# A two-layer hybrid decoder trunk on one core: loads of the decays by chunk, two products of the second layer moved into the end of the first, and operands of the way out ordered by halves of the tokens

## The chip, the cores and the metric

One core of one Trainium2 chip. A core has five engines that run side by side, each through its own instructions in order: TensorE (PE; its weight loads are listed as PEld), VectorE (DVE), ScalarE (ACT), GpSimd (POOL) and SyncE (SP), which here only issues DMA. The metric is the time of one execution in microseconds of the device (us); the comparison is of medians of runs.

## The reference

Two residual layers with RMSNorm and a last RMSNorm, on 1024 tokens of width 1024, all in float32. The first ("even") layer has dilated attention and an HGRN2 recurrence behind one projection; the second ("odd") is a gated DeltaNet with 8 key heads and 16 value heads. Cut to what the change touches:

```python
def forward(x):                                   # (1, 1024, 1024)
    h = x + even_mixer(rms_norm(x, norm_w[0]))    # ends in: concat(a, b) @ w_out
    h = h + odd_mixer(rms_norm(h, norm_w[1]))
    return rms_norm(h, final_norm_w)

def odd_mixer(hn):
    qkv, z, b_logit, a_logit = split(hn @ w_in)   # b_logit, a_logit: 16 columns each
    q, k, v = split(silu(causal_conv4(qkv)))
    g = -exp(a_log) * softplus(a_logit + dt_bias); gcum = cumsum(g within a chunk)
    decay = exp(where(causal, gcum_i - gcum_j, -inf))
    a_mat = I + where(strict, (k beta) @ k.T * decay, 0)      # solved per chunk and head
    ...                                           # delta rule over the chunks
    return (rms_norm(o) * silu(z)) @ w_out
```

## The kernel before

**Products.** Each float32 operand is split into `hi` (an ACT cast to fp32r) and `lo` (a DVE subtraction, `cut`, line 345); a product is three matmuls (`mm3`, line 382). Weights come in units of four loads of 256 KB through two `raw` buffers into seven `hi` and seven `lo` buffers; `unit()` (line 371) hands out a unit and loads the next. Accumulators of projections lie in two PSUM banks `pj`.

**Even layer** (line 555). Its way out, `out_proj` (line 491), goes through eight groups of 256 rows of the mixed activations, which lie in DRAM (`ymix`) and are cut into operands by `y_steps` (line 537) in four loads: two blocks of 128 rows (c) by two halves of 512 tokens. The first group of the even way out (`lead`) starts with tokens 512 to 1023; the other groups start with token 0. In the last group the finished tokens go on at once: the residual's sum on DVE, `norm_T` (line 449: square and root on ACT, scaling on DVE, eight transposes `nt` on PE, cast `hn_hi` on ACT, subtraction `hn_lo` on DVE). The order here is the framework's, by its estimates.

**Odd layer** (line 1049). All its operations are collected and put in order by `Plan` (line 82), a list scheduler with costs per operation; it takes 430 ns of SP and 3100 ns to the landing for every load (line 124), and holds a tile back until its predecessor in the same buffer is free (gates, line 212). The order it finds is what each engine then executes. `gates()` (line 1061) makes the cumulated decays: `ab`, a product of 32 columns (`abp`, half by half), a turn (`abt`), then ACT and DVE steps, and at the end a table `gcd` of 64 KB in DRAM, a row of 128 floats per chunk (8) and value head (16). `start()` (line 1511) makes the first keys (`pk0`, then `conv`), `proj(j)` the others. For each of the 8 key heads `invert(hh)` (line 1295) loads rows of `gcd` to all 128 partitions as L, two chunks of two heads per load; ACT does four Relu (one per chunk and head) and one exp per load; DVE multiplies L with `kk` from PE, a PSUM bank `c` per four chunks, of which there is one; then follow the inverse and `recur(hh)` (line 1397), which loads the same rows again by chunk as A (`decays`, line 1289), for POOL to add a mask. `invert(hh + 1)`, the projections and the gate products run as filling between the steps of `recur(hh)`. All loads and stores are issued by SP.

Of the kernel before, what the change touches and what calls it, by code (L numbers as in the profile page):

```python
# [10 lines left out]
F32 = mybir.dt.float32  # L11
# [8 lines left out]
P = 128  # L20
# [3 lines left out]
KC = D // P  # L24
# [57 lines left out]
class Plan:  # L82
# [87 lines left out]
    def edges(self):  # L170
# [28 lines left out]
        for op in ops:  # L199
            i = op["i"]  # L200
            for ap, w in [(z, True) for z in op["out"]] + [(z, False) for z in op["ins"]]:
                t = ap.tensor
# [9 lines left out]
        tags = {}  # L212
        for t, users in tiles.values():
            if getattr(t, "tag_meta", None) is not None:
                tags.setdefault((t.tag, t.tag_meta.bufs), []).append((t.owner_uid, sorted(set(users))))
        gates = []
        for (tag, bufs), ts in tags.items():
            ts.sort(key=lambda z: z[0])
# [93 lines left out]
def trunk_kernel(ctx: ExitStack, tc: tile.TileContext, x, ew, ewo, ow, owab, owo, nw, fnw, lbl, hnw,  # L312
# [13 lines left out]
    def bank(tag, shape, name):  # L326
        return pp.tile(shape, F32, name=name, tag=tag, bufs=BANKS[tag])
# [43 lines left out]
    def unit(first=lambda: None):  # L371
        w = ahead.pop() if ahead else load_unit()
        first()
        ahead.append(load_unit())
        return w
# [36 lines left out]
    def drain(fill):  # L412
        for _ in fill:
            pass
# [8 lines left out]
    def hn(part, k, s):  # L423
        return HN[part][k // 4][:, k % 4, s]
# [24 lines left out]
    def norm_T(src, t, sm, nwb, xn):  # L449
# [3 lines left out]
        for h in range(2):  # L453
# [4 lines left out]
            act.copy(hi, ps)  # L458
            dve.tensor_tensor(HN["lo"][h][:, :, t * 128:(t + 1) * 128], ps, hi.bitcast(F32), op=ALU.subtract)

    def proj_cols(w, c, name, evac, halves=(0, 1), mid=None):

        w = by_k(w[2 * c:2 * c + 2], 128)
        for half in halves:
            ps = bank("pj", [P, 512], f"{name}_{half}")
            s = slice(half * 512, half * 512 + 512)
            for k, (hi, lo) in enumerate(w):
                mm3(ps, hi, lo, hn("hi", k, s), hn("lo", k, s), k == 0, k == KC - 1)
                if k == KC - 1:
                    if mid and half == 0:  # L470
                        mid()
                    evac(s, ps)
                if k % 2:
                    yield 1.3
# [16 lines left out]
    def out_proj(groups, y_parts, hres, after, tags, lead=0.0, spread=False):  # L491
# [1 line left out]

        n_ = 0
        y = [y_parts(groups[0])]
        drain(y_steps(*y[0]))
        for g in groups:
            yh, yl = y.pop()[:2]
            steps = iter(())
# [34 lines left out]
                yield 1.3  # L534
            drain(steps)

    def y_steps(yh, yl, row, then=None):

        for c in range(2):
            for half in range(2):  # L540
                n = slice(half * 512, half * 512 + 512)
                cut(ymix[row + c * 128:row + c * 128 + 128, n], yh[c][:, n], yl[c][:, n], f"y{row}_{c}_{half}")
                yield
        if then:
            then()
# [9 lines left out]
    def even_layer(es):  # L555
# [482 lines left out]
            drain(fill)  # L1038
        open_stage("wy", WAY)
        drain(out_first(range(4, 8), ["pj", "b"]))  # L1040
        stage.close()

    with ExitStack() as es:
# [5 lines left out]
    def odd_layer(es):  # L1049
# [11 lines left out]
        def gates():  # L1061
# [7 lines left out]
            load_row(dt, dtb)  # L1069
            load_row(ea, alog)  # L1070
            act.activation(ea, ea, AF.Exp)

            w = unit().rearrange("p (k j) -> p k j", k=KC)
            ab = sp.tile([P, T], F32, name="ab", tag="LpQ")
            for half in range(2):
                p = bank("pj", [P, 512], f"abp{half}")
                s = slice(half * 512, half * 512 + 512)
                for k in range(2):
                    for r in range(4):
                        for part in ("hi", "lo"):  # L1080
                            pe.matmul(p[32 * r:32 * r + 32], w[:, 2 * r + k], hn(part, 2 * r + k, s).bitcast(F32),
                                      start=k == 0 and part == "hi", stop=k == 1 and part == "lo")
                act.copy(ab[:, s], p)
                yield (9 if not half else 0.0), 2.6
            yield 1.0, 0.0
            tp = bank("c", [P, NT, 32], "abt")
            for c in range(NT):
# [198 lines left out]
                    gated(7, e, h, G7[0][:, e, h, :])  # L1286
                    yield 0.7, 0.4

        def decays(hh, c):
            g = sp.tile([P, 2, 128], F32, name=f"A{hh}_{c}", tag="A", bufs=4)  # L1290
            sync.dma_start(g, bass.AP(tensor=gcd.tensor, offset=gcd.offset + (c * 16 + 2 * hh) * 128,
                                         ap=[[0, P], [128, 2], [1, 128]]))
            return g

        def invert(hh):
            kT = KT[hh]
# [3 lines left out]

            for c in range(0, NT, 2):

                sync.dma_start(L[:, 2 * c:2 * c + 4, :],
                               bass.AP(tensor=gcd.tensor, offset=gcd.offset + (c * 16 + 2 * hh) * 128,
                                       ap=[[0, P], [16 * 128, 2], [1, 256]]))
                for u in range(4):
                    act.activation(L[:, 2 * c + u, :], L[:, 2 * c + u, :], AF.Relu,
                                   bias=gt["ngc"][:, c + u // 2, 2 * hh + u % 2:2 * hh + u % 2 + 1])
                act.activation(L[:, 2 * c:2 * c + 4, :], L[:, 2 * c:2 * c + 4, :], AF.Exp, scale=-1.0)
# [87 lines left out]
        def recur(hh):  # L1397
# [2 lines left out]
            ss = SS[hh] = sp.tile([P, NT, 2], F32, name=f"oss{hh}", tag="oss", bufs=2)  # L1400

            def decay_a(c):
                DA = decays(hh, c)
                pool.tensor_tensor(DA, DA, MA[:, None, :].to_broadcast([P, 2, 128]), op=ALU.add)
                for e in range(2):
                    act.activation(DA[:, e, :], DA[:, e, :], AF.Exp, bias=gt["ngc"][:, c, 2 * hh + e:2 * hh + e + 1])
                return DA
# [101 lines left out]
                yield from g  # L1509

        def start():
            yield from conv(unit(), 0, 8, "k0", lambda: k_tile(0))
            yield from proj(0)

        fill = blend(plan.early(10000, gates()), start())
# [83 lines left out]
```

## Time and profile before

| | us |
|---|---|
| median of three runs | 2263.21 (2261.76 to 2263.47) |
| the profiled execution, its own time | 2265.53 |
| its span, from the first to the last instruction | 2263.8 |
| PE busy | 2159.7 |
| DVE busy | 1410.1 |
| ACT busy | 943.2 |
| mean granted clock of PE, share of full speed | 0.980 |

The page of the profile gives busy times, a picture of the span in 40 slices, DMA queues, the chain of work that ended last and groups of instructions. Matmuls overlap in the records: the spacing of their starts is the pace. In rows of a timeline the brackets hold the idle time before an instruction and what ended it; a wait that ends with a load names the load. L291 and L305 are the lines of the planner's and the lanes' calls, so that tiles, not lines, tell what an instruction is. The granted clock has two levels, 1.00 and 0.50 (2.4 and 1.2 GHz); a value between them is a mean over a stretch.

### The profile page before, as it was taken

Reading aid. Unit: us, or ns where it says so; the run is one execution under the profiler, and the core shown is the slowest. Engines: PE = TensorE matmul, PEld = TensorE weight load, DVE = VectorE, ACT = ScalarE, POOL = GpSimd, SP = SyncE. Lnnn points to the kernel's source line nnn. Section 1 sums busy time; section 2 is a strip of 40 time slices with the busy share of each in tenths; the row PEclk is TensorE's granted clock in tenths of the full one; section 3 lists DMA queues with packets and bytes.
Section 4 is the critical chain, followed back from the end, with each engine's and each line's share of the span. In section 5 each row is a group of like instructions: output and inputs, shape, how many; then the busy total and the mean of one; then the engine's idle time right before and its main releaser. Section 6 shows DMA issues by size and latency. Waiting matters only on the chain. (4 is left out here: it accounts for less than half of the span.)

```text
span 2263.8 us, 52378 instructions
## 1 busy us (share of the span) xinstructions
PE 2159.7 (95%) x21781; PEld 1777.9 (79%) x21781; DVE 1410.1 (62%) x3236; ACT 943.2 (42%) x2519; POOL 240.7 (11%) x252
## 2 busy tenths in 40 slices
PE   7999999999999999979998898989899999999998
PEld 6888888888877878757886786868787787887887
DVE  6353535353444344457675896969788787965677
ACT  6233333333232232222235755655565555553223
POOL 0010101010000000000000012121212122220100
PEclk9999999999999999989999999999999999999999
DMA  4111111114342334353222312231211222223223
GB/s 147 39 48 48 48 48 44 48 34 129 89 130 73 106 92 122 98 162 105 91 102 96 87 44 42 80 71 54 76 53 68 60 66 54 78 73 144 94 95 119
DMA packets 99566, 184.14 MB, mean 81 GB/s; under 512 B 12160, under 2 KB 29696, under 8 KB 99328
## 3 DMA queue, kind: packets, MB, share of 16 engines
q1 hardware_dynamic: 99328, 180.79, 26.4%
q8 instruction: 171, 2.80, 0.5%
q14 instruction: 67, 0.55, 0.1%
HBM read 151.25 MB, written 29.49 MB: 80 GB/s over the span
## 5 line engine op out<-in xcount | busy, mean ns | idle before, releaser
L305 DVE TENSOR_TENSOR w_lo<-raww,w_hi 128x512 fp32r<-128x512 f32 x160 | 117.8, 740 | 150.9 <-ACT w_hi L305 150.4
L305 ACT CAST w_hi<-raww 128x512 fp32r<-128x512 f32 x160 | 99.3, 621 | 204.2 <-DMA raww<-in_ewo_dram 54.2
L291 PE MATMUL op<-w_hi,yplo 128*128 128x512 f32 x448 | 140.1, 391 | 0.7 <-DVE hr L291 0.7
L305 ACT ACTIVATE P<-P,nm 128x256 f32<-128x256 f32 (+7 forms) x128 | 71.4, 559 | 133.8 <-DVE nm L305 133.7
L291 ACT CAST w_hi<-raww 128x512 fp32r<-128x512 f32 x132 | 81.3, 618 | 92.4 <-DMA raww<-in_owo_dram 38.1
L291 DVE TENSOR_TENSOR hr<-hr,op 128x512 f32<-128x512 f32 x128 | 87.4, 686 | 48.4 <-PE op L291 46.0
L305 PE MATMUL op<-w_hi,yphi 128*128 128x512 f32 x320 | 105.6, 403 | 9.9 <-DVE hres L305 6.6
L291 PE MATMUL oz<-hn_hi,w_hi 128*128 128x512 f32 x256 | 110.9, 433 | 0.0
L291 DVE TENSOR_TENSOR w_lo<-raww,w_hi 128x512 fp32r<-128x512 f32 x132 | 95.0, 724 | 24.6 <-ACT w_hi L291 22.4
L291 PE MATMUL pv<-hn_hi,w_hi 128*128 128x512 f32 x256 | 108.2, 422 | 0.0
L291 PE MATMUL oz<-hn_lo,w_hi 128*128 128x512 f32 x256 | 105.1, 410 | 0.0
L291 PE MATMUL oz<-hn_hi,w_lo 128*128 128x512 f32 x256 | 103.6, 405 | 0.0
L291 PE MATMUL pv<-hn_lo,w_hi 128*128 128x512 f32 x256 | 103.2, 403 | 0.0
L291 PE MATMUL pv<-hn_hi,w_lo 128*128 128x512 f32 x256 | 102.8, 402 | 0.0
L291 POOL TENSOR_TENSOR A<-A,MA 128x256 f32<-128x256 f32 x64 | 53.4, 836 | 447.7 <-DMA A<-gcd 217.5
L305 DVE STREAM_TRANSPOSE PB<-P 128x256 f32<-128x256 f32 (+3 forms) x64 | 54.6, 853 | 72.8 <-ACT P L305 72.8
L291 PEld LDWEIGHTS op<-w_hi,yplo 128*128 128x128 f32 x448 | 84.1, 188 | 18.3 <-DVE hr L291 0.9
L291 PE MATMUL op<-w_lo,yplo 128*128 128x512 f32 x224 | 87.2, 389 | 0.0
L305 DVE TENSOR_TENSOR hres<-hres,op 128x512 f32<-128x512 f32 x96 | 64.6, 682 | 31.2 <-PE op L305 30.4
L305 PEld LDWEIGHTS op<-w_hi,yphi 128*128 128x128 f32 x320 | 61.5, 193 | 26.0 <-DVE hres L305 7.8
L305 DVE CUSTOM_DVE_ANT_0 P<-S,G 128x256 f32<-128x256 f32 (+7 forms) x128 | 58.1, 491 | 36.5 <-PE S L305 36.1
L291 DVE SCALAR_TENSOR_TENSOR vT<-uv,cws,vT 128x512 f32<-128x512 f32 x96 | 73.7, 769 | 4.6 <-ACT vT L291 2.9
(345 smaller groups left out, 6348.8 us busy)
## 6 DMA issues: line engine op xcount, KB each, us to landing
raww<-in_ew_dram SPq DMA_DIRECT2D x128, 256.0 KB, 3.1
raww<-in_ow_dram SPq DMA_DIRECT2D x100, 256.0 KB, 3.0
V<-vd SPq DMA_DIRECT2D x64, 256.0 KB, 5.4
rawy<-ymix SPq DMA_DIRECT2D x64, 256.0 KB, 2.7
raww<-in_ewo_dram SPq DMA_DIRECT2D x32, 256.0 KB, 3.0
L<-gcd SPq DMA_DIRECT2D x32, 256.0 KB, 11.7
A<-gcd SPq DMA_DIRECT2D x64, 128.0 KB, 2.9
ymix<-oy SPq DMA_DIRECT2D x32, 256.0 KB, 2.4
```

The costliest lines, as they stand in the source:

```text
L291: ops[i]["f"](*ops[i]["a"], **ops[i]["kw"])
L305: return f(*a, **kw)
```

## The change

L's rows of `gcd` are loaded chunk by chunk: two loads of 128 KB where one of 256 KB brought two chunks; the Relu and exp steps stay. At the end of the even layer, behind its way out, the unit of `ab` and the unit of the first keys are taken (which loads that unit and the next), and the first halves of the two products are made: `ab` and `pk0`, tokens 0 to 511, each left in its `pj` bank. The odd layer copies them from there and makes the second halves; its planner no longer has those two products and the eight weight loads. The gates' first step now hands 5.0 instead of 9 units of filling to the blend. `y_steps` cuts by halves of the tokens first, and by blocks of rows inside; the first group with `lead` begins with the second half. The planner sorts the tiles of a tag by the number in their name.

```diff
@@ -212,7 +212,7 @@
         tags = {}
         for t, users in tiles.values():
             if getattr(t, "tag_meta", None) is not None:
-                tags.setdefault((t.tag, t.tag_meta.bufs), []).append((t.owner_uid, sorted(set(users))))
+                tags.setdefault((t.tag, t.tag_meta.bufs), []).append((int(t.name.rsplit("_", 1)[1]), sorted(set(users))))
         gates = []
         for (tag, bufs), ts in tags.items():
             ts.sort(key=lambda z: z[0])
@@ -458,12 +458,34 @@
             act.copy(hi, ps)
             dve.tensor_tensor(HN["lo"][h][:, :, t * 128:(t + 1) * 128], ps, hi.bitcast(F32), op=ALU.subtract)
 
+    def ab_half(w, half):
+
+        w = w.rearrange("p (k j) -> p k j", k=KC)
+        p = bank("pj", [P, 512], f"abp{half}")
+        s = slice(half * 512, half * 512 + 512)
+        for k in range(2):
+            for r in range(4):
+                for part in ("hi", "lo"):
+                    pe.matmul(p[32 * r:32 * r + 32], w[:, 2 * r + k], hn(part, 2 * r + k, s).bitcast(F32),
+                              start=k == 0 and part == "hi", stop=k == 1 and part == "lo")
+        return p
+
+
+    begun = {}
+
     def proj_cols(w, c, name, evac, halves=(0, 1), mid=None):
 
         w = by_k(w[2 * c:2 * c + 2], 128)
         for half in halves:
+            s = slice(half * 512, half * 512 + 512)
+            ps = begun.pop((name, half), None)
+            if ps is not None:
+                if mid and half == 0:
+                    mid()
+                evac(s, ps)
+                yield 1.3
+                continue
             ps = bank("pj", [P, 512], f"{name}_{half}")
-            s = slice(half * 512, half * 512 + 512)
             for k, (hi, lo) in enumerate(w):
                 mm3(ps, hi, lo, hn("hi", k, s), hn("lo", k, s), k == 0, k == KC - 1)
                 if k == KC - 1:
@@ -493,7 +515,7 @@
 
         n_ = 0
         y = [y_parts(groups[0])]
-        drain(y_steps(*y[0]))
+        drain(y_steps(*y[0], first=1 if lead else 0))
         for g in groups:
             yh, yl = y.pop()[:2]
             steps = iter(())
@@ -534,10 +556,10 @@
                 yield 1.3
             drain(steps)
 
-    def y_steps(yh, yl, row, then=None):
-
-        for c in range(2):
-            for half in range(2):
+    def y_steps(yh, yl, row, then=None, first=0):
+
+        for half in (first, 1 - first):
+            for c in range(2):
                 n = slice(half * 512, half * 512 + 512)
                 cut(ymix[row + c * 128:row + c * 128 + 128, n], yh[c][:, n], yl[c][:, n], f"y{row}_{c}_{half}")
                 yield
@@ -1038,6 +1060,12 @@
             drain(fill)
         open_stage("wy", WAY)
         drain(out_first(range(4, 8), ["pj", "b"]))
+
+        begun["ab"] = unit()
+        begun["ab", 0] = ab_half(begun["ab"], 0)
+        begun["k"] = unit()
+        proj = proj_cols(begun["k"], 0, "pk0", lambda s, ps: begun.update({("pk0", 0): ps}), (0,))
+        drain(proj)
         stage.close()
 
     with ExitStack() as es:
@@ -1069,19 +1097,13 @@
             load_row(dt, dtb)
             load_row(ea, alog)
             act.activation(ea, ea, AF.Exp)
-
-            w = unit().rearrange("p (k j) -> p k j", k=KC)
             ab = sp.tile([P, T], F32, name="ab", tag="LpQ")
+            w = begun.pop("ab")
             for half in range(2):
-                p = bank("pj", [P, 512], f"abp{half}")
+                p = begun.pop(("ab", half), None) or ab_half(w, half)
                 s = slice(half * 512, half * 512 + 512)
-                for k in range(2):
-                    for r in range(4):
-                        for part in ("hi", "lo"):
-                            pe.matmul(p[32 * r:32 * r + 32], w[:, 2 * r + k], hn(part, 2 * r + k, s).bitcast(F32),
-                                      start=k == 0 and part == "hi", stop=k == 1 and part == "lo")
                 act.copy(ab[:, s], p)
-                yield (9 if not half else 0.0), 2.6
+                yield (5 if not half else 0.0), 2.6
             yield 1.0, 0.0
             tp = bank("c", [P, NT, 32], "abt")
             for c in range(NT):
@@ -1286,11 +1308,9 @@
                     gated(7, e, h, G7[0][:, e, h, :])
                     yield 0.7, 0.4
 
-        def decays(hh, c):
-            g = sp.tile([P, 2, 128], F32, name=f"A{hh}_{c}", tag="A", bufs=4)
+        def decays(g, hh, c):
             sync.dma_start(g, bass.AP(tensor=gcd.tensor, offset=gcd.offset + (c * 16 + 2 * hh) * 128,
                                          ap=[[0, P], [128, 2], [1, 128]]))
-            return g
 
         def invert(hh):
             kT = KT[hh]
@@ -1300,9 +1320,8 @@
 
             for c in range(0, NT, 2):
 
-                sync.dma_start(L[:, 2 * c:2 * c + 4, :],
-                               bass.AP(tensor=gcd.tensor, offset=gcd.offset + (c * 16 + 2 * hh) * 128,
-                                       ap=[[0, P], [16 * 128, 2], [1, 256]]))
+                decays(L[:, 2 * c:2 * c + 2, :], hh, c)
+                decays(L[:, 2 * c + 2:2 * c + 4, :], hh, c + 1)
                 for u in range(4):
                     act.activation(L[:, 2 * c + u, :], L[:, 2 * c + u, :], AF.Relu,
                                    bias=gt["ngc"][:, c + u // 2, 2 * hh + u % 2:2 * hh + u % 2 + 1])
@@ -1400,7 +1419,8 @@
             ss = SS[hh] = sp.tile([P, NT, 2], F32, name=f"oss{hh}", tag="oss", bufs=2)
 
             def decay_a(c):
-                DA = decays(hh, c)
+                DA = sp.tile([P, 2, 128], F32, name=f"A{hh}_{c}", tag="A", bufs=4)
+                decays(DA, hh, c)
                 pool.tensor_tensor(DA, DA, MA[:, None, :].to_broadcast([P, 2, 128]), op=ALU.add)
                 for e in range(2):
                     act.activation(DA[:, e, :], DA[:, e, :], AF.Exp, bias=gt["ngc"][:, c, 2 * hh + e:2 * hh + e + 1])
@@ -1509,7 +1529,7 @@
                 yield from g
 
         def start():
-            yield from conv(unit(), 0, 8, "k0", lambda: k_tile(0))
+            yield from conv(begun.pop("k"), 0, 8, "k0", lambda: k_tile(0))
             yield from proj(0)
 
         fill = blend(plan.early(10000, gates()), start())
```

## Rows read from the trace of the kernel before

**Rows 1.** Part 1 of the page: busy time of each engine, its share of the span of 2263.8 us, and its instructions.
```profile
PE 2159.7 (95%) x21781; PEld 1777.9 (79%) x21781; DVE 1410.1 (62%) x3236; ACT 943.2 (42%) x2519; POOL 240.7 (11%) x252
```
**Rows 2.** The waits of PE from 1150 us to the end: who waited for whom, us in total, times, longest us.
```profile
PE kk L291 <- DVE L L291: 30.2, 12, 6.6
PE up L291 <- issue: 8.4, 1, 8.4
PE ot L291 <- POOL bv L291: 5.5, 1, 5.5
```
**Rows 3.** The timelines of ACT (three rows), DVE and PE (one each) in the train of L loads of the fifth head, 1582 to 1608 us: start, us, engine, line, operation, out<-in, shapes, and in brackets the idle time before it and what ended it.
```profile
1592.55 0.40 ACT L291 ACTIVATE L<-L,g_ngc 128x128 f32<-128x128 f32 x1 [0.43 <-DMA L<-gcd]
...
1597.93 0.40 ACT L291 ACTIVATE L<-L,g_ngc 128x128 f32<-128x128 f32 x1 [3.58 <-DMA L<-gcd]
...
1599.05 0.61 ACT L291 ACTIVATE uq<-q 128x512 f32<-128x512 f32 x1
1599.70 0.69 DVE L291 SCALAR_TENSOR_TENSOR q<-uq,q 128x512 f32<-128x512 f32 x1 [4.17 <-ACT uq L291]
1600.71 0.80 PE L291 MATMUL kk<-kT 128*128 128x128 f32 x2 [5.65 <-DVE L L291]
```
**Rows 4.** The timelines of ACT and PE in the trains of the next three heads, in the same columns: for each the release of the second load, of the third load, and PE's wait.
```profile
1699.29 0.40 ACT L291 ACTIVATE L<-L,g_ngc 128x128 f32<-128x128 f32 x1 [1.29 <-DMA L<-gcd]
...
1703.23 0.40 ACT L291 ACTIVATE L<-L,g_ngc 128x128 f32<-128x128 f32 x1 [2.14 <-DMA L<-gcd]
...
1706.00 0.79 PE L291 MATMUL kk<-kT 128*128 128x128 f32 x2 [4.91 <-DVE L L291]
...
1804.46 0.40 ACT L291 ACTIVATE L<-L,g_ngc 128x128 f32<-128x128 f32 x1 [1.24 <-DMA L<-gcd]
...
1810.06 0.40 ACT L291 ACTIVATE L<-L,g_ngc 128x128 f32<-128x128 f32 x1 [3.79 <-DMA L<-gcd]
...
1812.83 0.79 PE L291 MATMUL kk<-kT 128*128 128x128 f32 x2 [6.65 <-DVE L L291]
...
1911.73 0.40 ACT L291 ACTIVATE L<-L,g_ngc 128x128 f32<-128x128 f32 x1 [1.32 <-DMA L<-gcd]
...
1915.57 0.40 ACT L291 ACTIVATE L<-L,g_ngc 128x128 f32<-128x128 f32 x1 [2.04 <-DMA L<-gcd]
...
1918.34 0.80 PE L291 MATMUL kk<-kT 128*128 128x128 f32 x2 [5.13 <-DVE L L291]
```
**Rows 5.** Busy time by stretches at the border of the two layers: from:to, length, then PE, PEld, DVE, ACT and POOL busy with their instructions, granted clock of PE, share of the DMA engines, GB/s.
```profile
1193.70:1205.50 11.80, 9.04 (x57) 3.83 (x56) 7.35 (x11) 4.51 (x12) 0.00 (x0) 0.98 0.11 46
1205.50:1211.10 5.60, 1.89 (x8) 1.78 (x8) 1.33 (x5) 3.25 (x5) 0.00 (x0) 0.50 0.51 139
1211.10:1220.00 8.90, 8.89 (x31) 7.16 (x32) 2.91 (x5) 2.58 (x5) 0.00 (x0) 0.77 0.45 148
```
**Rows 6.** Parts 5 and 6 of the page. First two groups of instructions, the cast and the subtraction that make a weight's pair of operands (count, then busy us and mean ns, then idle before them); then two groups of loads (count, KB of each, median us from issue to landing).
```profile
L305 DVE TENSOR_TENSOR w_lo<-raww,w_hi 128x512 fp32r<-128x512 f32 x160 | 117.8, 740 | 150.9 <-ACT w_hi L305 150.4
L305 ACT CAST w_hi<-raww 128x512 fp32r<-128x512 f32 x160 | 99.3, 621 | 204.2 <-DMA raww<-in_ewo_dram 54.2
...
L<-gcd SPq DMA_DIRECT2D x32, 256.0 KB, 11.7
A<-gcd SPq DMA_DIRECT2D x64, 128.0 KB, 2.9
```
**Rows 7.** The views by tile: L from 1583 to 1608 us (four loads of one train), then A from 1259 to 1275 us (three loads behind the first train).
```profile
DMA to landing us min/median/max: 5.7/11.1/14.6
DMA to landing us min/median/max: 5.8/7.7/10.1
```
**Rows 8.** The timeline of SP's queue, 1582 to 1608 us and 1259 to 1275 us: start of the first issue, us to the end of the last, what, and how many.
```profile
1583.46 1.92 SPq L291 DMA_DIRECT2D L<-gcd  x4
...
1261.84 5.86 SPq L291 DMA_DIRECT2D A<-gcd  x3
```
**Rows 9.** The chain of work that ended last, three of its pieces: start, us, what, and how many instructions it merges.
```profile
1220.79 3.67 PE abp L291 x32
...
1485.89 8.39 issue
...
1542.18 2.75 PE pk L291 x12
```
**Rows 10.** Groups of instructions by line from 1193.7 to 1220 us: count, busy us and mean ns, idle before.
```profile
L291 PE MATMUL abp<-hn_lo,wab 128*32 128x512 f32 x16 | 4.0, 595 | 0.0
```
**Rows 11.** The timelines of PE (two rows), DVE and SP's queue at the border of the layers, 1180 to 1212 us.
```profile
1204.18 1.24 PE L305 MATMUL nt<-ident,xn 128*128 128x128 f32 x8 [2.68 <-DVE xn L305]
1208.74 1.89 PE L291 MATMUL abt<-gcs__14227,ab 128*128 128x32 f32 x8 [3.32 <-DMA gcs__14227<-in_dtb_dram]
...
1205.60 1.22 DVE L305 TENSOR_TENSOR hn_lo<-nt,hn_hi 128x512 fp32r<-128x512 f32 x2
...
1205.50 0.81 SPq L291 DMA_DIRECT2D gcs__14227<-in_cst_dram  x2
```
**Rows 12.** The timelines of PE (two rows) and DVE (one) at the start of the even layer's way out, 975 to 1000 us.
```profile
982.99 0.80 PE L305 MATMUL op<-w_hi,yphi 128*128 128x512 f32 x1 [2.75 <-ACT yphi L305]
...
994.93 0.79 PE L305 MATMUL op<-w_hi,yphi 128*128 128x512 f32 x1 [6.62 <-DVE hres L305]
...
993.59 0.69 DVE L305 TENSOR_TENSOR yphi<-rawy,yphi 128x512 fp32r<-128x512 f32 x1 [8.00 <-ACT yphi L305]
```

## Prediction

> **What bounds the kernel now.** I read the page first: TensorE (PE) is busy for 2159.7 of 2263.8 us [rows 1]. So a microsecond is won only where PE stands still or runs at its lower clock, and the second view is PE's waits. Behind 1150 us they are few and long. The largest, 30.2 us, is the product `kk` of `invert`, which waits for VectorE's (DVE) work on L; one of 8.4 us is put down to nothing ("issue"), and one of 5.5 us is for GpSimd (POOL) [rows 2]. The third view is the timeline around the four longest `kk` waits, which come once per head from the fifth head on. The reader is to see one chain there. ScalarE (ACT) runs in order and stands at the first Relu of L's third load, released at 1597.93; the tanh `uq<-q` behind it starts at 1599.05, DVE's `q` at 1599.70, and PE's `kk` at 1600.71 after 5.65 us of standing still [rows 3]. The same order returns three times with waits of 4.91, 6.65 and 5.13 us [rows 4]: 22.3 us in the four heads. The fourth view is the border between the layers, by stretches: from 1193.7 to 1220.0 us PE has 31 `pk` products, 32 `abp`, 24 transposes and 8 `abt` to do; it is busy for 19.8 of 26.3 us, and its clock is at the lower level (0.50, that is 1.2 GHz) from 1205.5 to 1211.1 [rows 5].
>
> **L's decays by chunk.** Removed: 32 loads of 256 KB; added: 64 of 128 KB, the same bytes. Alone, loads of this size from `gcd` (the A loads) land in 2.9 us in the median, the 256 KB ones in 11.7 [rows 6]. That is no saving of 8.8 us per load, for the four stand in a row: in one train they landed 5.7 us (the shortest) to 14.6 us (the longest) after their issue [rows 7], the last being issued some 1.4 us after the first [rows 8]; so a train moves 1 MB in about 16 us, and eight halves of it are still 1 MB. I take the rate of these rows and let a chunk land where half of its pair had. What is then won is the wait for the pair's other half. Chunk 4 opens the third pair. It lands half way between the second and the third release, and the chain of [rows 3] hangs on it: (1597.93 - 1592.55) / 2 = 2.7 us, and in the next three 2.0, 2.8 and 1.9 us [rows 3, 4]. Sum 9.4 us. All four are less than the waits they shorten (4.9 us and more), so they reach PE whole, if ACT's order stays. For the other heads' smaller `kk` waits (30.2 - 22.3 = 7.9 us) I take 1 us. The 8.4 us of "issue" and the wait for POOL I leave: the first falls inside a train (from 1485.89) and shows no releaser [rows 9], the second hangs on an A load behind a train, whose end doesn't move. **10.4 us.** The price: SP issues 32 loads more, 0.4 to 0.5 us each, in the same train in which the ring is full anyway; who is queued behind them on SP is the A load, and before it a weight load in some heads.
>
> Bounds: the nearest rows for a train of small loads are three A loads, issued from 1261.84 on, the last one finished issuing at 1267.70; they took 10.1, 7.7 and 5.8 us [rows 7, 8], so they landed within about 1 us of each other, 0.5 us apart. Eight chunks at that pace behind a first one of 2.9 us are in at 6.5 us; chunk 4 is there at 5 us, before the first pair of today, and the 22.3 us go whole, with 4 to 8 us more in the first heads: 30. At the other end every chunk costs the lone 2.9 us: chunk 4 at 14.5 us, when today's third load is released (1597.93 - 1583.46 = 14.5), and the last at 23.2 instead of 16.0. I take the rate of the trains because the A loads of [rows 8] were behind other loads, which had cleared the way for them. So from 30 us won to 25 us lost (priced with the rivals), with 10.4 won in between.
>
> The Trainium skill ("DMA: Bandwidth & Descriptors", section "Rules for kernel authors") speaks against this edit: many small transfers are to be coalesced into one large one; the page's fit, 2.0 us fixed plus bytes over 436 GB/s (for another path of issue), makes 2.6 us of 256 KB and, by estimate, 4.6 us of two halves one after the other. By it the edit costs 2.0 us per pair. The rows show neither: 256 KB took 5.7 us and more here.
>
> **The first products.** PE did half of this already: all 32 `abp` of the first half, 16 of them in this row, stand in the stretch before 1220 [rows 10], in the even layer's tail. New there are the 24 products of `pk0`'s first half (12 cost 2.75 us, so 5.5 us) and the two units' eight weight loads. Today's tail, at full clock, would take: `abp` 3.7 us for 32; transposes 3 x 1.24 = 3.7; `abt` 1.89 / 2 = 0.9; `pk` 31 x 2.75 / 12 = 7.1 [rows 5, 9, 11]. That is 15.4 of 26.3 us: 10.9 us are lost. They are lost because the last transposes come at 1204.18 with 2.68 us of wait, `abt` after 3.32 us for a load that SP had held until 1205.50 (the odd layer's first tile gets its place only then), and the weights stand behind that load on SP [rows 11]. Changed, PE has 3.7 + 5.5 + 3.7 = 12.9 us of work from 1193.7 to 1206.8, when the second half of hn is complete (`hn_lo`, 1205.60 + 1.22); then the second halves of both products follow at once, since their weights are there. I keep 3.0 us lost: the PSUM banks wait for two ACT copies into tiles of the odd layer, 1 us; and eight casts (0.62 us) and eight subtractions (0.74 us) [rows 6] go into the tail. ACT has room for 5.0 us (7.3 idle in the first stretch), DVE not quite for 5.9 (11.8 - 7.35 = 4.45 idle) [rows 5]; 1.5 us of it delay the norm, and 0.5 us I add for order. **10.9 - 3.0 = 7.9 us.** Bounds: 10.4 if nothing delays the norm, 2 if all of DVE's 5.9 us stand ahead of it. Whether the gates then end earlier I count at nothing: PE's other products cover it.
>
> **The way out by halves.** The even way out starts with tokens 512 on. Today it waits 2.75 us for the fourth operand; with that half loaded first, the wait goes. What is late next is there already: PE waits 6.62 us at 994.93 for the residual's sum, which DVE does behind a cut whose load comes late (8.00 us idle to 993.59) [rows 12]. PE reaches the same point sooner and waits longer. **0**, at most 2.7. The odd way out's first group gains the same way where its loads are long done: 0. The planner's new sort key orders the same tiles: 0.
>
> **Sum:** 10.4 + 7.9 = 18.3 us. The profiled execution took 2265.5 us (span 2263.8 and 1.7 around it), 0.1% above the median of the three timed runs, 2263.2; the term is the same for both: 2247.2 on it, and 2244.9 as the median. Forecast **2245**.
>
> **Rivals.** *The trains get faster.* If what held a 256 KB load was its two pieces 8 KB apart per partition, and not the bytes, chunks land as in [rows 8]: 30 + 7.9, so 2225, or with the 8.4 and 5.5 us of [rows 2] gone as well 2211; I name it 2218. For: a lone 128 KB load takes a quarter of a 256 KB load's median. Against: nothing in these rows shows a train of them from a standing start. *Only one term comes.* The odd layer is put in order by a planner that believes every load lands 3.1 us after its issue; another order of ACT can put the same Relus ahead of other work, or the eight casts can hold up the norm: 2253 to 2255, say 2254. *It doesn't do what it says.* `abp` stood in the tail already, `pk0` is put behind the transposes where no time is left, and chunk 4 still waits behind chunk 5's order on ACT: 2261. *Slower: each chunk pays for itself.* Place: the seven trains (the first holds two heads). The eighth chunk lands later than today's last load, and the A load behind it with it, from a spacing of (16.0 - 2.9) / 7 = 1.9 us on; at 2.9 us they are 7.2 us late, and if half of that reaches PE in seven trains it costs 25 us, while chunk 4 wins nothing any more: 2263.2 + 25 - 7.9 = 2280. At 2.5 us the loss (15 us) equals what chunk 4 and the border win (6 + 7.9), so this is the point. The A loads of rows 8, which overlap, speak against it. The page named above is on this side; the trace so far bears it out in nothing but the lone load's 2.9 us.
>
> **How the numbers follow.** Forecast 45% (its own range 2236 to 2254), faster trains 18%, one term 20%, nothing 7%, slower 10%. A measurement of this kernel can tell about 0.2%, 4.5 us, from no change, so faster means under 2258.7. Faster: 45 + 18 + most of the 20 less a few that miss, 79%; same: the 7 and a little of the 20, 10%; slower 11%. The range leaves out the slower case and the fastest part of the first rival: 2214 to 2262.
>
> **What would show it.** Right: eight chunks per head landing evenly over 16 us; ACT's wait for the third pair split in two; the four `kk` waits at 2.2 to 3.9 us instead of 4.9 to 6.7; `pk0` between the transposes before 1205, and no wait over 1 us at 1205 to 1212, with the clock at 1.00 there; the wait at 995 as long as now plus 2.7. Wrong: chunks landing within 7 us (then the `kk` waits are gone), chunks 2.9 us apart, or a norm that ends well after 1207.

## The result, and the profile after

The changed kernel took 2253.0 us in the median of five runs (2252.19 to 2256.83), the kernel before 2263.47 (2261.76 to 2267.2) beside it. These two medians lie 10.5 us apart; the ratio on record is 0.9945, 95% interval 0.9934 to 0.9957, which is 12.4 us less (9.7 to 14.9). From here on "us less" is worked out from such ratios on record, which differ a little from the ratios of the medians. A second set of runs gave 0.9940 (0.9928 to 0.9953). The forecast was 2245, that is 18.3 us less. The profiled execution of the changed kernel spans 2250.4 us, 13.4 less than the one before.

The page of the profile after, part 1 (PE's busy time is what it was, [rows 1]) and part 6 (L's loads; [rows 6] has those before):

```profile
PE 2159.4 (96%) x21781; PEld 1776.3 (79%) x21781; DVE 1417.3 (63%) x3236; ACT 945.3 (42%) x2519; POOL 247.3 (11%) x252
...
L<-gcd SPq DMA_DIRECT2D x64, 128.0 KB, 9.4
```

A load of half the size lands in 9.4 us where the whole one took 11.7. The waits of PE from 1150 us to the end, which answer to [rows 2] (who waited for whom, us in total, times, longest us):

```profile
PE kk L291 <- DVE L L291: 21.8, 13, 4.0
PE pq L291 <- issue: 8.6, 1, 8.6
PE vp L291 <- DVE A L291: 4.9, 4, 2.3
...
PE ot L291 <- POOL bv L291: 3.6, 1, 3.6
```

`kk` lost 8.4 us of its 30.2, the wait on "issue" is still there, and `vp`'s wait for DVE's A, 0.6 us in all before, has grown to 4.9. The timelines of ACT, DVE and PE in the train of the fifth head ([rows 3] before):

```profile
1580.86 0.40 ACT L291 ACTIVATE L<-L,g_ngc 128x128 f32<-128x128 f32 x1 [1.12 <-DMA L<-gcd]
...
1583.51 0.69 ACT L291 ACTIVATE L<-L,g_ngc 128x128 f32<-128x128 f32 x2 [1.44 <-DMA L<-gcd]
1585.56 0.40 ACT L291 ACTIVATE L<-L,g_ngc 128x128 f32<-128x128 f32 x1 [1.35 <-DMA L<-gcd]
...
1586.68 0.61 ACT L291 ACTIVATE uq<-q 128x512 f32<-128x512 f32 x1
...
1587.32 0.69 DVE L291 SCALAR_TENSOR_TENSOR q<-uq,q 128x512 f32<-128x512 f32 x1 [4.06 <-ACT uq L291]
...
1588.33 0.80 PE L291 MATMUL kk<-kT 128*128 128x128 f32 x2 [3.55 <-DVE L L291]
```

It is the same chain as before: Relu, `uq`, `q`, `kk`. Chunks now release ACT one by one, in these rows 2.1 and 2.7 us apart, and the Relu that `uq` stands behind comes 12.4 us after the train's first issue (1573.19) instead of 14.5. PE's waits in the next three heads ([rows 4] before):

```profile
1693.53 0.79 PE L291 MATMUL kk<-kT 128*128 128x128 f32 x2 [3.89 <-DVE L L291]
...
1799.06 0.80 PE L291 MATMUL kk<-kT 128*128 128x128 f32 x2 [3.97 <-DVE L L291]
...
1809.36 0.71 PE L291 MATMUL vp<-bv,L 128*128 128x128 f32 x4 [2.30 <-DVE A L291]
...
1904.90 0.79 PE L291 MATMUL kk<-kT 128*128 128x128 f32 x2 [3.65 <-DVE L L291]
...
1914.99 0.71 PE L291 MATMUL vp<-bv,L 128*128 128x128 f32 x4 [2.08 <-DVE A L291]
```

The four `kk` waits are 15.1 us instead of 22.3. The border between the layers by stretches, in the columns of [rows 5]:

```profile
1193.70:1205.50 11.80, 11.80 (x75) 7.74 (x68) 10.17 (x16) 7.02 (x13) 0.00 (x0) 1.00 0.33 118
1205.50:1211.10 5.60, 5.60 (x41) 2.46 (x40) 0.92 (x4) 1.96 (x4) 0.00 (x0) 1.00 0.47 104
1211.10:1220.00 8.90, 8.02 (x44) 6.63 (x43) 4.03 (x10) 8.71 (x13) 0.00 (x0) 1.00 0.23 80
```

PE is busy for 25.4 of the 26.3 us, at full clock throughout; the one wait left is 0.88 us for ACT's copy `uk`.

**Where the time went.** The same matmuls run in all kernels, so the start of one can be set against the start of the same one (same tile, same count) in the profiled execution before. The table has these leads at eight places, in us (minus: earlier than before), for the changed kernel and for runs that follow. Ahead of the way out, at 963, no part of the change has run yet, and what stands there is how executions differ; so only differences along a row count. At 1225 the order of the products isn't the same in the runs with the border part (neighbours there lead by 11.0 to 14.2 us in the changed kernel); counted by all columns multiplied so far, the lead is 11.0.

| time before | 963 | 1043 | 1188 | 1225 | 1310 | 1591 | 1994 | 2140 |
|---|---|---|---|---|---|---|---|---|
| changed kernel | +1.7 | -0.5 | -0.9 | -11.1 | -9.7 | -10.3 | -11.5 | -12.7 |
| changed, once more | +2.1 | +0.4 | -0.3 | -10.4 | -9.3 | -9.6 | -11.1 | -13.0 |
| L by chunk alone | +1.3 | +0.9 | +0.8 | +2.3 | +1.9 | +0.2 | -2.2 | -2.9 |
| border alone | +2.0 | +0.3 | +0.2 | -9.9 | -3.0 | -1.6 | -1.8 | -1.0 |
| way out alone | +1.2 | -0.5 | -0.9 | -0.9 | -1.3 | -1.0 | -1.8 | -3.1 |
| changed, L whole | +1.1 | -2.2 | -2.1 | -12.2 | -5.7 | -4.2 | -4.3 | -5.5 |
| changed, table at 9 KB | -0.1 | -1.9 | -1.3 | -11.5 | -15.2 | -37.3 | -64.2 | -64.6 |
| before, table at 9 KB | +1.0 | -0.7 | -0.9 | -0.9 | -7.8 | -26.6 | -53.5 | -54.7 |

In the changed kernel the border wins 10.2 us between 1188 and 1225 (10.1 in its second execution). The stretch with the four long trains, 1591 to 1994, wins 1.2 us (1.5 in the second), though the `kk` waits in it are 7.3 us shorter.

### The profile page after: what moved, and what is told of

Its sections match the earlier page's. It is cut to its first block, busy times and chain, and to the rows that moved or that the text cites. A ratio compares the mean times of both kernels' runs of the same rounds, so it can differ in the third digit from the quotient of the medians.

```text
span 2250.4 us, 52461 instructions
## 1 busy us (share of the span) xinstructions
PE 2159.4 (96%) x21781; PEld 1776.3 (79%) x21781; DVE 1417.3 (63%) x3236; ACT 945.3 (42%) x2519; POOL 247.3 (11%) x252
## 4 chain that ended last, share of the span: by engine, by line
PE 82%; DVE 7%; DMA 6%; ACT 2%; issue 2%; SPq 1%; POOL 0%; DVEq 0%; ACTq 0%; POOLq 0%
PE op L291 8%; PE op L305 7%; PE oz L291 7%; PE pv L291 6%; PE avp L305 4%; PE bq L305 4%; PE ak L305 4%; PE aq L305 4%; PE ag L305 4%; PE bf L305 4%; PE bip L305 4%; PE bg L305 3%; PE pk L291 3%; PE o L305 3%; PE S L305 3%; DMA L<-gcd 2%
## 5 line engine op out<-in xcount | busy, mean ns | idle before, releaser
L305 PE MATMUL op<-w_hi,yphi 128*128 128x512 f32 x320 | 104.7, 401 | 10.1 <-DVE hres L305 9.7
L291 PEld LDWEIGHTS op<-w_hi,yplo 128*128 128x128 f32 x448 | 84.1, 188 | 18.3 <-DVE hr L291 0.9
L305 POOL TENSOR_TENSOR ay<-ay,sg 128x512 f32<-128x512 f32 x16 | 20.1, 1278 | 498.6 <-DMA ay<-rdd 498.6
```

What stands on the lines that cost most here:

```text
L291: ops[i]["f"](*ops[i]["a"], **ops[i]["kw"])
L305: return f(*a, **kw)
```

## The experiments

**The parts alone.** Four runs, each part's edit taken from the diff of the change: L's loads alone, the two first products alone, the order of the operands alone, and the changed kernel with L's loads whole again:

```diff
-                decays(L[:, 2 * c:2 * c + 2, :], hh, c)
-                decays(L[:, 2 * c + 2:2 * c + 4, :], hh, c + 1)
+                sync.dma_start(L[:, 2 * c:2 * c + 4, :],
+                               bass.AP(tensor=gcd.tensor, offset=gcd.offset + (c * 16 + 2 * hh) * 128,
+                                       ap=[[0, P], [16 * 128, 2], [1, 256]]))
```

> The kernel before with nothing changed but L's loads, chunk by chunk. Theory A (the gain of a shorter wait is given back): chunk 4 lands half an interval earlier, the kk waits of heads 5 to 8 fall by 7 us in all, but PE gets only 1 to 2 of them, because the lower clock lasts as long as before and so runs on into work, and because the A load behind the train lands no earlier and becomes the next wait (vp for DVE's A); with the first heads 1 to 4 us less than before: 2259 to 2262 us, ratio 0.998 to 0.9995. Theory B (the term was right, the border's was too large): 7 to 10 us less, 2253 to 2256 us, ratio 0.9955 to 0.997.

> The kernel before with the two first products in the even layer's end alone (L whole, operands of the way out by blocks of rows; the planner's sort key, which alone leaves every engine's order as it was, is kept since the order is not found without it). Theory A: nearly all of the gain is here: 8 to 10 us less, 2253 to 2255 us. Theory B: 3 to 4 us less, about 2260.

> The kernel before with the operands of the way out by halves alone. The prediction's 0: 2263 us, and the wait for the residual's sum near 995 longer by what the wait near 983 gives up. Rival, from the profile after: 1 to 2.5 us less, since PE gets through this stretch 2.2 us sooner there.

> The changed kernel with L's loads put back to two chunks each. Theory A: 1 to 4 us more than the changed kernel, so 2254 to 2257 us, and no vp wait for A over 1 us in heads 7 and 8. Theory B: 7 to 10 us more, 2260 to 2263.

> The changed kernel once more, beside the others: ratio 0.9945 as before, so about 12 us less than the kernel before. Its distance to the runs with one part gives what the parts are worth together: the parts alone measured 0.9975, 0.9974 and 0.9992, which add up to 0.994.

Measured, beside a kernel before of 2267.2 us (2265.9 for the last):

| | us, median | ratio, 95% interval | us less |
|---|---|---|---|
| L by chunk alone | 2261.55 | 0.9975 (0.9960 to 0.9989) | 5.7 (2.5 to 9.1) |
| border alone | 2261.31 | 0.9974 (0.9961 to 0.9986) | 5.9 (3.2 to 8.8) |
| way out alone | 2264.65 | 0.9992 (0.9983 to 1.0001) | 1.8 (-0.2 to 3.9) |
| changed, L whole | 2257.62 | 0.9957 (0.9944 to 0.9969) | 9.7 (7.0 to 12.7) |
| changed, once more | 2251.84 | 0.9940 (0.9928 to 0.9953) | 13.6 (10.6 to 16.3) |

Neither theory holds as it was put. L is worth 4 to 6 us (alone, or from 0.9957 to 0.9940) and the border 6 alone, where theory A had 1 to 4 and 8 to 10, and theory B 7 to 10 and 3 to 4. The parts alone add up to 13.4 us, which within the noise is what the whole measured (12.4 and 13.6); so the times show no loss or gain by putting the parts together. L's 4 us out of the whole are not clear of noise either, since the two intervals overlap. The table of leads shows what becomes of the border's part in the profiled executions: the border wins its 10 us by 1225 in every run that has it, and gives 6.5 to 6.9 of them back by 1310 if L comes whole, but 1.4 if it comes by chunk. The place is the first train. With L whole, the timelines of SP's queue, of ACT and of PE ("changed, L whole"):

```profile
1235.83 7.17 SPq L291 DMA_DIRECT2D L<-gcd  x4
1243.04 2.56 SPq L291 DMA_DIRECT2D A<-gcd  x1
1245.70 2.67 SPq L291 DMA_DIRECT2D raww<-in_ow_dram  x1
...
1257.32 0.62 ACT L291 CAST w_hi<-raww 128x512 fp32r<-128x512 f32 x1 [4.21 <-DMA raww<-in_ow_dram]
...
1259.35 0.79 PE L291 MATMUL pv<-hn_hi,w_hi 128*128 128x512 f32 x1 [5.32 <-ACT uv L291]
```

A weight load stands on SP behind the second head's L and an A; ACT waits for it, `uv` stands behind that cast, and PE waits 5.32 us. In the changed kernel the planner has put the weight load behind the first chunk of that train, and the wait is 0.96 us (timelines of SP's queue and PE):

```profile
1236.55 2.70 SPq L291 DMA_DIRECT2D L<-gcd  x1
1239.35 1.11 SPq L291 DMA_DIRECT2D raww<-in_ow_dram  x1
1240.52 6.29 SPq L291 DMA_DIRECT2D L<-gcd  x7
...
1254.53 0.50 PE L291 MATMUL pv<-hn_hi,w_hi 128*128 128x512 f32 x1 [0.96 <-ACT uv L291]
```

So two parts that the prediction added up work on one place. What this is worth in the median is not shown: by the times, what L brings beside the border (4 us) is no more than what it brings alone (6).

**Is A what is late next?** In the changed kernel, the A loads go out two chunks ahead:

```diff
-                DA = ahead_a.pop()
-                if c < NT - 1:
-                    ahead_a.append(decay_a(c + 1))
+                DA = ahead_a.pop(0)
+                if c < NT - 2:
+                    ahead_a.append(decay_a(c + 2))
...
-            ahead_a = [decay_a(0)]
+            ahead_a = [decay_a(0), decay_a(1)]
```

> The changed kernel with the A loads issued two chunks ahead instead of one, so that the one that stood behind the train of L's chunks stands before it. Theory A (A behind the train is what is late next): the vp waits of 2.30 and 2.08 us in heads 7 and 8 are gone, and what heads 5 to 8 win grows from 1.2 to 4 or 5 us: 3 to 4 us less than the changed kernel. Rival (the wait moves on to ACT's exp of A or to a weight load that is now behind the train): no difference over 1 us.

2252.28 us, ratio 0.9943 (0.9930 to 0.9955): no difference. The waits for A are 5.0 us in all, as they were (4.9), only elsewhere: 3.34 us in the fifth head, 0.85 in the seventh. The rival's time holds, though the wait moved neither to ACT's exp nor to a weight load: another A load now stands behind the train, and POOL and DVE come to `vp` as late as before (the rows for this are shown further down). That a load behind the train is what is late next is borne out; that it matters which one is not.

**What makes a train slow?** The prediction took the bytes of the trains at their rate, and both theories of the next two texts (C and D) hold that L stays slow as long as its pieces are the same. For this the table got another order of its rows, with a head pair's eight chunks one after the other, and loads of one or of four chunks:

```diff
-            sync.dma_start(gcd, cs[:, 3, :])
+            for e in range(2):
+                sync.dma_start(bass.AP(tensor=gcd.tensor, offset=gcd.offset + e * 128, ap=[[256, 8], [2048, 8], [1, 128]]),
+                               cs[e::2, 3, :])
...
-            sync.dma_start(g, bass.AP(tensor=gcd.tensor, offset=gcd.offset + (c * 16 + 2 * hh) * 128,
-                                         ap=[[0, P], [128, 2], [1, 128]]))
+            n = g.shape[1]
+            sync.dma_start(g, bass.AP(tensor=gcd.tensor, offset=gcd.offset + (hh * 16 + 2 * c) * 128,
+                                         ap=[[0, P], [128, n], [1, 128]]))
```

> The changed kernel with the table of decays in the order of the head pairs (two stores instead of one), and L still loaded by chunk, 128 pieces of 1 KB each. Both theories: trains as now (13 to 16 us for 1024 pieces), and the time of the changed kernel within 3 us.

> The same table, and L in two loads of four chunks, 128 pieces of 4 KB each: the same 1 MB in 256 pieces instead of 1024. Theory C (what limits a train is the number of its pieces, about 78 per us; the pieces of 1 KB themselves keep the 16 engines busy for only 3.4 us of some 17): both loads are in 4 to 6 us after the first issue, the kk waits of heads 5 to 8 (15.1 us) and the vp waits (4.4) go, and the wait of 8.6 us near 1476 with them: 20 to 30 us less than the changed kernel, 2223 to 2235 us. Theory D (what limits it is the bytes, or that all partitions read one row): the train takes 13 to 16 us as now, chunk 4 comes with the last, and the time is that of the changed kernel or up to 10 us more.

The first, meant as the control, took 2199.75 us, ratio 0.9714 (0.9699 to 0.9729): 65 us less than before. The second took 2203.06, ratio 0.9726 (0.9708 to 0.9744). Theories C and D both fall with the control: bytes, pieces and their size are those of the changed kernel, all partitions of a load still read one row, and the trains (one head's eight loads, where the trace has the last landing), from the first issue to the last landing, take 6.8 to 8.1 us instead of 14.6 to 21.4. What had changed is where the rows lie. Before, the eight rows that a train reads (1 KB each) lay 8 KB apart, in the new order 1 KB. But the store was in two parts too, and the planner had found another order. One more edit has neither, the changed kernel with a padded table:

```diff
-    gcd = dp.tile([P, 128], F32, name="gcd")
+    gcd = dp.tile([P + 16, 128], F32, name="gcd")
...
-            sync.dma_start(gcd, cs[:, 3, :])
+            sync.dma_start(bass.AP(tensor=gcd.tensor, offset=gcd.offset, ap=[[18 * 128, 8], [128, 16], [1, 128]]), cs[:, 3, :])
...
-            sync.dma_start(g, bass.AP(tensor=gcd.tensor, offset=gcd.offset + (c * 16 + 2 * hh) * 128,
+            sync.dma_start(g, bass.AP(tensor=gcd.tensor, offset=gcd.offset + (c * 18 + 2 * hh) * 128,
```

> The changed kernel with one thing else: the table of decays has 9 KB from a chunk's rows to the next chunk's instead of 8 KB (1 KB of padding). Every engine's order is that of the changed kernel; bytes, pieces and loads are the same. Theory E (the eight rows of a train are read one behind the other because they lie 8 KB apart; with rows 1 KB apart, in the run before, they were read side by side): trains in 6 to 8 us instead of 13 to 16, kk waits of heads 5 to 8 under 1 us, 2198 to 2206 us. Theory F (it was the two stores, or the planner's other order, that made the trains fast): trains as in the changed kernel, 2250 to 2256 us.

> The same with 12 KB from a chunk's rows to the next's. Theory E in a sharper form (what counts is the distance modulo 8 KB: two of the eight rows share a place, or rather four share each of two places): trains about half as long as now, 7 to 9 us, and 2205 to 2225 us. If any distance but 8 KB does: as with 9 KB. Theory F: as the changed kernel, 2250 to 2256 us.

> The changed kernel with L loaded two chunks at a time again, and the table at 9 KB. Theory E: the split into chunks is worth little once the rows are read side by side: within 3 us of the run with 9 KB and chunks. Theory F: as without the padding, about 2256 us.

> The kernel before with only the table's pitch changed to 9 KB. Theory E: the four kk waits of 22.3 us, the wait of 8.4 us near 1494 and that for POOL of 5.5 us go, with their half clock: 40 to 52 us less than before, 2214 to 2226 us, and the border's 8 to 10 us are what is left to the change. Theory F: 2263 to 2267 us.

For 12 KB, 18 is 24 and the table is longer; the other two have the same edit without L by chunk, and in the kernel before. Measured beside a kernel before of 2265.8 us:

| | us, median | ratio, 95% interval |
|---|---|---|
| changed, 9 KB | 2200.87 | 0.9711 (0.9691 to 0.9730) |
| changed, 12 KB | 2200.09 | 0.9710 (0.9690 to 0.9731) |
| changed, L whole, 9 KB | 2200.46 | 0.9707 (0.9688 to 0.9725) |
| before, 9 KB | 2211.24 | 0.9752 (0.9732 to 0.9771) |

What theory E forecast holds, for the kernel before with a little more than it said (2211 against 2214 to 2226): 1 KB of padding after every 8 KB is worth some 52 us to the changed kernel and 56 (52 to 61) to the kernel before. The order of the instructions on every engine is the same with 8, 9 and 12 KB, so theory F is out. That the rows are read one behind the other, as theory E words it, is not shown; that their distance decides is. The view by tile of L, around the train of the fifth head, with 8, 9 and 12 KB (in the second, three of the eight landings are missing from the trace):

```profile
DMA to landing us min/median/max: 3.4/9.8/13.6
```
```profile
DMA to landing us min/median/max: 2.9/3.4/3.5
```
```profile
DMA to landing us min/median/max: 3.1/5.1/5.5
```

and the same train by stretches with 8 KB (from the first issue on) and with 9 KB, in the columns of [rows 5]:

```profile
1573.00:1591.00 18.00, 14.45 (x69) 12.02 (x68) 10.76 (x30) 10.61 (x29) 0.00 (x0) 0.89 0.25 82
```
```profile
1546.00:1554.00 8.00, 8.00 (x44) 6.70 (x43) 6.14 (x13) 5.64 (x17) 0.00 (x0) 1.00 0.58 183
```

All loads together moved 82 GB/s, and now 183, and PE is busy all the time. With 9 KB, the `kk` waits are 5.4 us in all, none over 0.5, and no wait on "issue" is left among the longer ones (the page's waits of PE, 9 KB):

```profile
PE kk L291 <- DVE L L291: 5.4, 12, 0.5
PE tk L291 <- DVE kT L291: 5.1, 1, 5.1
PE vp L291 <- ACT oq L291: 3.7, 1, 3.7
```

With 12 KB the trains are slower than with 9 (8.7 to 10.8 us against 6.8 to 8.7), as the sharper form had it, but its time missed: with trains of some 9 us hardly anybody waits for them any more (`kk` 6.0 us in all, 1.1 the longest). And the split into chunks is worth nothing when the trains are fast (0.9707 against 0.9711), while the two other parts keep their size: from 2211.24 to 2200.46, 10.8 us (9.7 with 8 KB).

## Why the prediction came out as it did

The range, the sign and the forecast's own range (2236 to 2254) held, though both terms were too large: the sum was 18.3 us where 12.4 (9.7 to 14.9) came. Step by step:

**L by chunk, 10.4 us: the mechanism was right, the worth was not.** Chunks came at the old rate, trains of 16.8 to 17.9 us in heads 5 to 8 against 15.7 to 17.0, and the four `kk` waits fell by 7.3 us (2.1, 1.0, 2.7 and 1.5) where 9.4 were counted. What failed is the sentence "All four are less than the waits they shorten, so they reach PE whole". PE got 1.2 us of the 7.3 by 1994, and 2.4 in the run with L alone. Two things took the rest. One is the load behind the train: the text says of another wait that it hangs on an A load whose end doesn't move, and did not ask who waits for the same load in these four heads. `vp` did, 2.30 and 2.08 us in heads 7 and 8, by way of POOL and DVE (their timelines after, in the seventh head; the last row is the same subtraction in the fifth head, when POOL isn't at work on `bv`):

```profile
1801.89 0.75 POOL L291 TENSOR_TENSOR A<-A,MA 128x256 f32<-128x256 f32 x1 [21.48 <-DMA A<-gcd]
1802.59 5.84 POOL L291 TENSOR_TENSOR bv<-bv,ors 128x512 f32<-128x512 f32 x4
...
1807.45 1.52 DVE L291 TENSOR_TENSOR w_lo<-raww,w_hi 128x512 fp32r<-128x512 f32 x1
1808.90 0.41 DVE L291 TENSOR_TENSOR A<-qk,A 128x256 f32<-128x256 f32 x1
...
1603.66 0.68 DVE L291 TENSOR_TENSOR w_lo<-raww,w_hi 128x512 fp32r<-128x512 f32 x1
```

POOL adds the mask when the A load lands and goes on with `bv`; beside `bv`, DVE's subtraction takes 1.52 us instead of 0.68, and DVE comes to the step that `vp` waits for 7 us after the landing. In the kernel before `vp` starts 7.7 us after POOL's mask, in the changed one 7.5: what stands behind the load's end moved only as far as the load did. With the A loads two chunks ahead POOL's `bv` still stands behind the mask of the one that lands last, which fits the missing difference there.

The other is the clock. By stretches in the fifth head, before and after (columns as in [rows 5]; the second row of each is PE's work behind the wait at the lower clock, the third the work behind that):

```profile
1597.50:1600.70 3.20, 0.00 (x0) 0.00 (x0) 0.95 (x2) 2.77 (x8) 0.00 (x0) 0.50 0.24 75
1600.70:1604.00 3.30, 3.29 (x9) 2.71 (x10) 2.46 (x7) 3.30 (x9) 2.63 (x3) 0.50 0.00 0
1604.50:1606.00 1.50, 1.50 (x9) 1.27 (x8) 1.50 (x3) 0.67 (x3) 1.50 (x2) 1.00 0.00 0
```
```profile
1587.00:1588.30 1.30, 0.00 (x0) 0.00 (x0) 0.96 (x2) 0.98 (x3) 0.00 (x0) 0.50 0.24 87
1588.30:1593.50 5.20, 5.17 (x13) 4.20 (x14) 4.01 (x10) 4.70 (x12) 1.93 (x2) 0.50 0.14 46
1594.00:1596.00 2.00, 2.00 (x12) 1.66 (x11) 2.00 (x3) 0.04 (x1) 2.00 (x2) 1.00 0.16 40
```

The wait was shorter, but PE then worked for 5.2 us at 0.50 instead of 3.3: 1.9 us more at half pace cost 0.9 of the 2.1 us won. In the sixth head it is the same (PE works for 6.0 us at 0.50 behind the wait where it was 4.1), so nothing is left of the 1.0 us there; in heads 7 and 8 that work is no longer than before (2.9 us in each, 3.1 and 3.4 before), and `vp` alone takes the gain. Together these account for the 7.3 us: about 1.5 to the clock, 4.4 to `vp`, 1.2 won. The time of L is better than this stretch (3.9 us from 0.9957 to 0.9940, not clear of noise); that it also keeps the border's gain at the first train is seen in the leads.

**The first products, 7.9 us: mis-sized low at the place, high at the end.** From 1188 to 1225 they won 10.2 us, near the upper bound of 10.4: of the 3.0 us kept back only the wait of 0.88 us for ACT's copy came, the norm was not delayed (`hn_lo` ends at 1205.6, before at 1206.8), and `pk0` filled the gaps between the transposes, at full clock. What was missed is "PE's other products cover it" of what comes behind. The first train starts 13.7 us sooner (1228.83 against 1242.50), and the weight load behind the train is then what PE waits for (5.3 us with L whole); a wait `tk` for DVE's kT comes with it as well, 2.1 us with L whole and 2.4 in the changed kernel where it was 0.2. So alone the part is worth 5.9 us. That the changed kernel kept most of the gain at this place hangs on where the planner put that weight load among L's smaller ones, which the prediction did not foresee: that much is luck. By their own terms the bounds should have been 9.4 and 3.5: the upper one also leaves out the 1 us for the banks, the lower one counts the norm's 1.5 us twice.

**The way out, 0:** not separated. The wait moved as described. Both waits of PE in [rows 12] are now for the residual's sum (timeline of PE after):

```profile
987.47 0.79 PE L305 MATMUL op<-w_hi,yphi 128*128 128x512 f32 x1 [5.83 <-DVE hres L305]
994.25 0.80 PE L305 MATMUL op<-w_hi,yphi 128*128 128x512 f32 x1 [3.86 <-DVE hres L305]
```

9.7 us against 2.75 and 6.62. The part alone measured 1.8 us less (-0.2 to 3.9), and from 963 to 1043 the table's runs with it win 1.7 to 3.3 us, those without it 0.4 to 1.7; one run that isn't in the table has it and loses 1.0 us there.

**The sort key, 0:** no run has it alone; that it leaves every engine's order unchanged is only said beside the run of the border.

**The rivals.** "The trains get faster" did not happen here, but its mechanism lay next to the real one: the pieces' distance of 8 KB counts, but cutting a load in two doesn't take it away, for the next load's row lies 8 KB on as well. Its price (30 us, or 44 with the other two waits of [rows 2]) was too small beside the 52 and 56 measured, for a fast train also ends much of the lower clock. The sum left the wait on "issue" aside since it showed no releaser; all runs with slow trains have it at 7.5 to 8.6 us, with 9 KB in the kernel before and with 12 KB it is 2.1, and in the changed kernel with 9 KB none is over 0.3, so it hangs on the train. The traces say more: PE stops at the same place of its program each time (behind the 17153rd to 17155th of its matmuls, be the next one `up` or `pq`), and goes on 1.1 to 1.5 us after a packet of the queue that the page lists as "instruction" has ended. So PE seems to wait there for its own instructions, which come late during a slow train; no run changes this alone. "Each chunk pays for itself", with the Trainium skill's "DMA: Bandwidth & Descriptors", section "Rules for kernel authors", on its side, did not happen: twice the loads made a train about 1 us longer in all (16.8 to 17.9 against 15.7 to 17.0). That rule names transfers under 64 KB as mostly overhead, and both sizes here are larger. By the fixed 2.0 us of the same page of the Trainium skill (section "Anatomy of one DMA — SWDGE (gpsimd) path", so for another path of issue), four loads more, one after the other, would by estimate make it 8 us longer; the runs show that they don't.

A row that could have raised the question was in the trace of before. The first head's last load lands at 1257.8, the second head's first at 1261.1, and where the one train goes over into the other the rate is more than twice what it is ahead of that (stretches of the kernel before):

```profile
1249.00:1256.00 7.00, 6.20 (x30) 4.78 (x28) 3.85 (x17) 3.85 (x12) 0.00 (x0) 1.00 0.39 86
1256.50:1258.00 1.50, 0.74 (x6) 0.74 (x6) 0.70 (x3) 0.58 (x3) 0.00 (x0) 1.00 0.75 237
```

The two heads' rows lie 1 KB beside each other's; that this makes the rate is a guess from the later runs. Loads of both heads had been issued in the first stretch too, and it is as slow as a lone train.

## What to carry to other kernels

Before a wait is shortened, look at what else hangs on the same queue, and at how long PE's clock stays low behind the wait: of 7.3 us taken off four waits here, 1.2 reached the end of their stretch. Where two parts meet at one queue, measure each alone and taken out of the whole; here the parts alone added up to the whole within the noise (13.4 us against 12.4 and 13.6), and it took the leads in the traces to see that they meet. And where a queue is slow while the DMA engines are mostly idle (a share of 0.25 in the stretch with 8 KB), change where the data lie before changing how the loads are cut: 1 KB of padding was worth 52 us, four times the change.

## What the runs showed of the hardware

Eight loads in a row that each read one row of DRAM to 128 partitions landed in 6.8 to 8.7 us with the rows 9 KB apart, in 8.7 to 10.8 at 12 KB and in 14.6 to 21.4 at 8 KB (1 KB apart: 6.8 to 8.1), with the same bytes and pieces; a single such load (A) takes 2.9 to 3.0 us in the median in all of them. What in the memory makes the distance count, and which other distances do it, no run tells: 2, 4 and 16 KB weren't tried. DVE's subtraction of 128x512 took 1.52 us beside POOL's `bv` and 0.68 without it.
